# Token sums as split ones products, earlier z gates and 512-token split value products in a hybrid decoder layer on one core

## The chip, the core and the metric

The kernel runs on one core of a Trainium2 chip. The core has a matrix engine (PE; its weight loads are listed apart as PEld), a vector engine (DVE), a scalar engine (ACT), a GpSimd engine (POOL) and a sync engine (SP) that here only issues transfers. Each engine takes its instructions strictly in the order of its own program and waits for the others through semaphores. The metric is device time in microseconds (us) of one execution of the whole layer, as the median of several runs. A profile is one further execution with every instruction's start and duration recorded; L429 means line 429 of the kernel before.

## What is computed

One decoder layer over 2048 tokens of width 1024: RMS norm, one combined projection, three branches, a gated merge, an output projection and the residual. Cut to what the change touches:

```python
kk = heads(k * k_k); kk = kk / max(norm(kk, axis=-1), 1e-12)      # branch A: sum of squares over 64 channels
...
q = rope(rms_norm(q.reshape(t, 8, 64), q_g), pos)                 # branch B: sum of squares over 64 channels
p = softmax(concat([q @ kband.T * 64**-0.5 (masked), sink]))[..., :-1]
y_b = (p @ vband) * silu(z_b)
...
q = rms_norm(q.reshape(t, 4, 128), xq_g)                          # branch C: sum of squares over 128 channels
p = softmax(q @ km.T * 128**-0.5)                                 # 256 memory tokens
y_c = (p @ vm) * silu(z_c)
...
x = x + (g0*(y_a @ Wa) + g1*(y_b @ Wb) + g2*(y_c @ Wc)) @ w_out
```

Branch A is RWKV-7 time mixing with 8 heads of 64 channels, branch B sliding-window attention with 8 query heads, branch C cross attention with 4 heads into 256 memory tokens.

## The kernel before

The sequence is worked in four superblocks of TB = 512 tokens. Activations stand transposed, channels on the 128 partitions and 512 tokens along the free axis, so a sum over a head's channels is a sum over partitions.

All large products are float32 products made of three dense ones (`gemm3`, L425 to L431): each operand is split into a rounded high part and the remainder (type F32R), and high by high, high by low and low by high are accumulated. The high part is an ACT copy, the low part a DVE subtraction. Weights are loaded and split in the first superblock (L411, L412), written back to memory and read in split form (`whl`) later. Products with plain F32 operands (token sums, transposes, attention's probabilities times values, the recurrence) are left to the PE's own float32 path: the trace shows two instructions for each such matmul in the program.

`tok_stat` (L468) makes the sums of squares: for each of the four 128-token tiles the squares are the stationary operand and a narrow matrix of ones (`bones`, 128x2, for two heads of 64; `ones1`, 128x1, for one head of 128) is the moving one. Tokens come out on partitions. It is called once for each pair of heads in `rwkv_prep` (L669), once for each cross head (L899), once for each pair of heads in `swa_pair` (L996), and for the keys. A few narrow DVE instructions carry the sums into place (L673, L901, L998); POOL raises them to the power -0.5 (`rpow`, L398).

`cross_head` (L886) loads the head's keys `km` and values `vm` by SP transfers, projects and splits the queries, makes scores, the softmax with ACT (L918), scales the probabilities (L930), transposes them with PE (L932), copies them out of PSUM with ACT (L934) and multiplies by the values in plain F32, 256 tokens at a time (L936). Then `silu2` projects the z gate (24 dense products, a tanh on ACT, one DVE instruction) and L939 multiplies. `swa_pair` (L982) ends in the same way: transposes (L1042), value products (L1052), then `silu2` (L1056) and the multiplication L1057.

The program is written as two generators, `stream_r` (branch A: preparation, a triangular inverse on DVE, a recurrence of eight steps for two pairs of heads at a time) and `stream_f` (cross heads, window attention, the merges and gates). `weave` interleaves them by the numbers they yield. This only sets ranks: `order` (L276) then lays out every engine's instructions anew. `lay_out` keeps a clock for each engine, gives each instruction a cost by formula (`cost_PE`, `cost_DVE` and so on), lets buffers of a name be taken in program order only when one is free, and among the instructions that could start takes the one of lowest rank. What comes out is a fixed order on PE, DVE, ACT, POOL and SP. Dense projections that wait for nothing fill PE between the links of the dependent work.

Buffers that matter: `g2` (11 of 128x512), `rt` (6), `gt` (2, for gates), PSUM tiles `mm` (2, projections), `rw` (2, branch A), `as_` (2, attention), `oo` (1, attention output).

Of the kernel before, what the change touches and what calls it, by code (L numbers as in the profile page):

```python
# [19 lines left out]
TB = 512  # L20
NG = 11
NRT = 6
SCRATCH = 1024
RAW = 3
C = 64
NC_ = TB // C
# [258 lines left out]
def build(tc, A, nsb=4):  # L285
    nc = tc.nc
# [18 lines left out]
    def g2(dt=F32, shape=(128, TB)):  # L305
        return gp_.tile(list(shape), dt, name="g2")
# [52 lines left out]
    def pcol(name, i=0):  # L359
        o, w = PV[name]  # L360
        return pv[:, o + i:o + i + 1]
# [106 lines left out]
    def tok_stat(sq, nh, ntile, out):  # L468
        rhs = bones if nh == 2 else ones1
        for i in range(ntile):  # L470
            PE.matmul(out[:, i * nh:(i + 1) * nh], sq[:, i * 128:(i + 1) * 128], rhs, start=True, stop=True)
# [4 lines left out]
    V.memset(ones1, 1.0)  # L476

# [61 lines left out]
    Vd = dp.tile([128, 2, 512], F32, name="mv")  # L539
# [9 lines left out]
    def mem_kv(mT):  # L549
# [48 lines left out]
        for i in range(2):  # L598
            t = g2()
            S.activation(t, o[i], AF.Copy)  # L600
            nc.sync.dma_start(Vd[:, i], t)
# [10 lines left out]
    def chunks(t):  # L612
        return t.rearrange("p (c t) -> p c t", t=C)
# [9 lines left out]
    def tmp(tag="rt", bufs=NRT):  # L623
        return rp.tile([128, TB], F32, name=tag, bufs=bufs)
# [5 lines left out]
    def rwkv_prep(p, i, Z, dk, Nc, sb, hT, lwla, group):  # L630
# [35 lines left out]
        sq = tmp()  # L666
        S.activation(sq, k, AF.Square, scale=pcol("k_k", p))
        st = rw_ps()
        tok_stat(sq, 2, 4, st)  # L669
        sums, own = st[:, :8].rearrange("p (a e) -> p a e", e=2), dk[:, i].rearrange("p (a o) -> p a o", o=2)  # L670
        for e, h in ((0, EV), (1, OD)):
            for o, at in ((0, EV), (1, OD)):
                V.tensor_scalar(own[h, :, o], sums[at, :, e], 1e-24, None, op0=ALU.max)  # L673
# [195 lines left out]
    def silu2(blk, hT):  # L869

        o = proj(blk, hT)
        t = g2()
# [13 lines left out]
    def cross_head(h, sb, hT, yh, yl):  # L886
        km = rp.tile([128, 2, M], F32R, name="km", bufs=2)
        nc.sync.dma_start(km.bitcast(F32), Kd[h])
        vm = rp.tile([128, 2, 128], F32, name="vm", bufs=2)
        nc.sync.dma_start(vm, Vd[:, :, h * 128:(h + 1) * 128])  # L890
# [33 lines left out]
        yield 5.667  # L924
        oo = o_ps()
        for t2 in range(2):
            pt = s_ps().rearrange("p (k i t) -> p k i t", k=2, i=2)
            for i in range(2):
                q = 2 * t2 + i
                V.tensor_scalar(prs[t2][:, i], prs[t2][:, i], dn[:, q:q + 1], None, op0=ALU.mult)  # L930
                for kt in range(2):
                    PE.transpose(pt[:, kt, i], prs[t2][:, i, kt * 128:(kt + 1) * 128], ident)  # L932
            pts = g2(shape=(128, 2, 256))
            S.activation(pts.rearrange("p k t -> p (k t)"), pt.rearrange("p k i t -> p (k i t)"), AF.Copy)  # L934
            for kt in range(2):
                PE.matmul(oo[:, t2 * 256:(t2 + 1) * 256], vm[:, kt], pts[:, kt], start=kt == 0, stop=kt == 1)  # L936
        yield 3
        z = silu2(B_ZC + h, hT)
# [43 lines left out]
    def swa_pair(j, sb, hT, yh, yl):  # L982
# [49 lines left out]
        yield 4  # L1032
        Ps = []
# [22 lines left out]
        z = silu2(B_ZB + j, hT)  # L1056
# [245 lines left out]
```

## Time and profile before

| | us |
|---|---|
| median of 3 runs | 2292.9 (2291.53 to 2294.29) |
| the profiled execution | 2291.46 |
| its span, first to last instruction | 2289.7 |
| DVE busy in the span | 1481.7 |
| ACT busy in the span | 901.1 |

The profiled execution's time is 1.8 us more than its span. A PE instruction's listed duration includes the part of the pipeline that overlaps its successor: a dense 512-column product is listed with some 390 ns, yet the next starts about 230 ns later. What a product costs on PE is therefore read from the distance between starts, not from its duration.

### The profile page before, as it was taken

Reading aid. Unit: us, or ns where it says so; the run is one execution under the profiler, and the core shown is the slowest. Engines: PE = TensorE matmul, PEld = TensorE weight load, DVE = VectorE, ACT = ScalarE, POOL = GpSimd, SP = SyncE. Lnnn points to the kernel's source line nnn. Section 1 sums busy time; section 2 is a strip of 40 time slices with the busy share of each in tenths; the row PEclk is TensorE's granted clock in tenths of the full one; section 3 lists DMA queues with packets and bytes.
Section 4 is the critical chain, followed back from the end, with each engine's and each line's share of the span. In section 5 each row is a group of like instructions: output and inputs, shape, how many; then the busy total and the mean of one; then the engine's idle time right before and its main releaser. Section 6 shows DMA issues by size and latency. Waiting matters only on the chain.

```text
span 2289.7 us, 37168 instructions
## 1 busy us (share of the span) xinstructions
PE 2251.8 (98%) x13900; PEld 1832.9 (80%) x13900; DVE 1481.7 (65%) x3798; ACT 901.1 (39%) x1971; POOL 149.5 (7%) x209
## 2 busy tenths in 40 slices
PE   8999999999999999999999999999999999999999
PEld 6878778778788788878888878887887887887887
DVE  7799789774458766953435966784244696686312
ACT  6654564545243443433214344332222434434210
POOL 1000110000000010000000001000000001000000
PEclk9999999999999999999999999999999999999999
DMA  7766556589834344446773433445675434343555
GB/s 241 265 210 230 174 178 222 208 288 335 312 135 159 128 140 152 152 155 232 236 254 125 152 122 135 149 148 186 230 251 184 152 131 165 120 153 117 210 193 192
DMA packets 146227, 430.56 MB, mean 188 GB/s; under 512 B 16641, under 2 KB 21121, under 8 KB 146049
## 3 DMA queue, kind: packets, MB, share of 16 engines
q1 hardware_dynamic: 129920, 398.83, 50.4%
q10 hardware_dynamic: 16128, 29.37, 3.8%
q8 instruction: 110, 1.80, 0.3%
q14 instruction: 69, 0.56, 0.1%
HBM read 333.24 MB, written 94.90 MB: 187 GB/s over the span
## 4 chain that ended last, share of the span: by engine, by line
PE 82%; DVE 10%; DMA 3%; ACT 2%; issue 2%; POOL 2%; SPq 0%; ACTq 0%; DVEq 0%; POOLq 0%
PE mm L429 20%; PE mm L431 20%; PE mm L430 19%; PE rw L706 2%; PE rw L827 1%; DVE whl L412 1%; PE oo L1052 1%; PE rw L820 1%; PE mm L1100 1%; PE oo L936 1%; PE mm L1098 1%; PE mm L1099 1%; PE rw L812 1%; POOL var L398 1%; DMA g<-in_x 1%
## 5 line engine op out<-in xcount | busy, mean ns | idle before, releaser
L429 PE MATMUL mm<-hH,whl 128*128 128x512 f32 x1888 | 753.3, 399 | 0.6 <-ACT gt L1065 0.6
L431 PE MATMUL mm<-hH,whl 128*128 128x512 f32 x1888 | 750.9, 398 | 0.0
L430 PE MATMUL mm<-hL,whl 128*128 128x512 f32 x1888 | 749.1, 397 | 0.0
L431 PEld LDWEIGHTS mm<-hH,whl 128*128 128x128 f32 x1888 | 355.6, 188 | 71.7 <-issue 0.7
L429 PEld LDWEIGHTS mm<-hH,whl 128*128 128x128 f32 x1888 | 355.9, 189 | 70.7 <-ACT gt L1065 1.2
L430 PEld LDWEIGHTS mm<-hL,whl 128*128 128x128 f32 x1888 | 355.7, 188 | 69.1 <-issue 0.5
L411 ACT ACTIVATE whl<-raw 128x512 fp32r<-128x512 f32 x178 | 112.3, 632 | 173.6 <-PE mm L431 98.2
L412 DVE TENSOR_TENSOR whl<-raw,whl 128x512 fp32r<-128x512 f32 x178 | 124.5, 701 | 62.3 <-ACT whl L411 61.2
L429 PE MATMUL mm<-yh,whl 128*128 128x512 f32 x384 | 152.0, 396 | 0.8 <-DVE g L1080 0.7
L430 PE MATMUL mm<-yl,whl 128*128 128x512 f32 x384 | 152.0, 396 | 0.0
L431 PE MATMUL mm<-yh,whl 128*128 128x512 f32 x384 | 150.8, 393 | 0.0
L818 ACT ACTIVATE SP<-Z,Pl 64x64 f32<-64x64 f32 x256 | 89.0, 348 | 117.2 <-DVE Z L828 113.6
L754 DVE STREAM_SHUFFLE ibc<-Nc 128x496 f32<-128x496 f32 (+30 forms) x248 | 113.7, 474 | 0.0
L755 DVE TENSOR_TENSOR ibc<-ibc,Yi 128x496 f32<-128x496 f32 (+30 forms) x248 | 104.9, 423 | 4.2
L1027 ACT ACTIVATE g<-g,mxs,st 128x256 f32<-128x256 f32 (+1 forms) x128 | 74.9, 588 | 79.2 <-DVE mxs L1020 78.9
L1080 DVE SCALAR_TENSOR_TENSOR g<-g,mm 128x512 f32<-128x512 f32 x32 | 21.9, 686 | 128.3 <-PE mm L431 128.3
L756 DVE TENSOR_TENSOR Yi<-Yi,ibc 128x496 f32<-128x496 f32 (+30 forms) x248 | 104.0, 419 | 1.4
L828 DVE SCALAR_TENSOR_TENSOR Z<-rw,Pl,SP 64x64 f32<-64x64 f32 x224 | 63.4, 283 | 44.3 <-PE rw L827 40.7
L429 PEld LDWEIGHTS mm<-yh,whl 128*128 128x128 f32 x384 | 72.1, 188 | 16.9 <-DVE g L1080 1.3
L430 PEld LDWEIGHTS mm<-yl,whl 128*128 128x128 f32 x384 | 72.2, 188 | 14.6
L431 PEld LDWEIGHTS mm<-yh,whl 128*128 128x128 f32 x384 | 72.1, 188 | 14.3
L824 DVE TENSOR_TENSOR Z<-rw,dk 64x128 f32<-64x128 f32 x128 | 36.8, 288 | 64.6 <-PE rw L820 54.5
(1815 smaller groups left out, 3718.3 us busy)
## 6 DMA issues: line engine op xcount, KB each, us to landing
whl<-k SPq DMA_DIRECT2D x486, 512.0 KB, 3.3
k<-whl SPq DMA_DIRECT2D x162, 512.0 KB, 3.2
raw<-in_w_in SPq DMA_DIRECT2D x118, 256.0 KB, 3.7
g<-in_x ACTq DMA_DIRECT2D x32, 256.0 KB, 4.3
out<-g ACTq DMA_DIRECT2D x32, 256.0 KB, 4.0
raw<-in_w_proj SPq DMA_DIRECT2D x24, 256.0 KB, 3.7
rt<-in_x ACTq DMA_DIRECT2D x24, 256.0 KB, 4.9
rt<-in_xt ACTq DMA_DIRECT2D x24, 256.0 KB, 5.7
```

What stands on the lines that cost most here:

```text
L411: S.activation(w[:, 0], raw, AF.Copy)
L412: V.tensor_tensor(w[:, 1], raw, w[:, 0].bitcast(F32), op=ALU.subtract)
L429: PE.matmul(out, lh, rh, start=i == 0, stop=False)
L430: PE.matmul(out, lh, rl, start=False, stop=False)
L431: PE.matmul(out, ll, rh, start=False, stop=i == n - 1)
L706: m = PE.matmul(g[:, c], BK[h, c0 + c], Q[h, c0 + c], start=True, stop=True)
L754: V.stream_shuffle(bc[:, :, :w], N_[:, :, s + 1:], [s] * 32)
L755: V.tensor_tensor(bc[:, :, :w], bc[:, :, :w], Y[:, :, s:s + 1].to_broadcast([128, n, w]), op=ALU.mult)
L756: V.tensor_tensor(Y[:, :, s + 1:], Y[:, :, s + 1:], bc[:, :, :w], op=ALU.add)
L818: S.activation(SP[h, i], Z[h, i, e, c], AF.Copy, scale=g[4][h, c:c + 1])
L828: upds = [V.scalar_tensor_tensor(Sst[h, g[0]] if c == NC_ - 1 else Z[h, i, e, c + 1], pS[h, i, e], g[4][h, c:c + 1], SP[h, i], op0=ALU.mul ...
L1027: S.activation(prs[b][:, i, m0:], prs[b][:, i, m0:], AF.Exp, scale=r2[:, b, i:i + 1], bias=mx[:, b, i:i + 1], accum_out=mx[:, b, 2 + i:3 + i])
```

## The change

Four edits, all inside `build`:

1. In superblocks 1 to 3 (`sb >= FIRST`; the first superblock keeps `tok_stat`) the token sums of `rwkv_prep`, `cross_head` and `swa_pair` become `spread_sums`: the squares are split into high and low (ACT copy, DVE subtraction) and are the moving operand of two dense products of 512 columns with a 128x128 matrix of ones (`ones2` in two blocks of 64, or `onesw`) as the stationary one. Every partition of the PSUM tile then holds the sum. To bring tokens to partitions, `half_sums` multiplies the PSUM tile by an identity pattern (`eye64`) and reduces over each chunk of 64; the cross heads use four `tensor_tensor_reduce` with `ident`. The sums of the sliding window's keys (L960) and of the memory keys stay.
2. In all four superblocks the cross heads' values are kept split (`Vd` and `vm` twice as large, `vm` with one buffer instead of two). The probabilities of all 512 tokens are transposed into two PSUM tiles, split, and multiplied by `gemm3` in six dense products of 512 columns in place of four plain ones of 256.
3. In `cross_head` the z gate's result goes to a `gt` buffer instead of a `g2`.
4. In `swa_pair` `silu2` stands ahead of the transposes in the program, not behind the value products.

```diff
+FIRST = 1
...
+    def spread_sums(out, w, sq, hi, lo):
+        S.activation(hi, sq, AF.Copy)
+        V.tensor_tensor(lo, sq, hi.bitcast(F32), op=ALU.subtract)
+        PE.matmul(out, w, hi, start=True, stop=False)
+        PE.matmul(out, w, lo, start=False, stop=True)
+    def half_sums(d, out, junk):
+        j = chunks(junk)
+        V.tensor_tensor(j, chunks(out), eye64.unsqueeze(1).to_broadcast([128, NC_, 64]), op=ALU.mult)
+        V.tensor_reduce(d, j, axis=AX.X, op=ALU.add)
...
-    Vd = dp.tile([128, 2, 512], F32, name="mv")
+    Vd = dp.tile([128, 2, 2, 512], F32, name="mv")
...
         for i in range(2):
-            t = g2()
-            S.activation(t, o[i], AF.Copy)
-            nc.sync.dma_start(Vd[:, i], t)
+            t = [g2(F32R), g2(F32R)]
+            S.activation(t[0], o[i], AF.Copy)
+            V.tensor_tensor(t[1], o[i], t[0].bitcast(F32), op=ALU.subtract)
+            for u in range(2):
+                nc.sync.dma_start(Vd[:, u, i], t[u].bitcast(F32))
...
         st = rw_ps()
-        tok_stat(sq, 2, 4, st)
+        if sb >= FIRST:
...
+            spread_sums(st, ones2, sq, *(rp.tile([128, TB], F32R, name="rt", bufs=NRT) for _ in range(2)))
+            half_sums(dk[:, i], st, sq)
+            V.tensor_scalar(dk[:, i], dk[:, i], 1e-24, None, op0=ALU.max)
...
-        vm = rp.tile([128, 2, 128], F32, name="vm", bufs=2)
-        nc.sync.dma_start(vm, Vd[:, :, h * 128:(h + 1) * 128])
+        vm = rp.tile([128, 2, 2, 128], F32R, name="vm", bufs=1)
+        nc.sync.dma_start(vm.bitcast(F32), Vd[:, :, :, h * 128:(h + 1) * 128])
...
-        tok_stat(sq, 1, 4, st)
-        V.tensor_copy(rs[:, :4], st[:, :4])
+        if sb >= FIRST:
+            spread_sums(st, onesw, sq, *(g2(F32R), g2(F32R)))
+            for i in range(4):
+                tk = slice(i * 128, (i + 1) * 128)
+                V.tensor_tensor_reduce(sq[:, tk], st[:, tk], ident, 1.0, 0.0, ALU.mult, ALU.add, rs[:, i:i + 1])
...
+        for q in range(4):
+            pr = prs[q // 2][:, q % 2]
+            V.tensor_scalar(pr, pr, dn[:, q:q + 1], None, op0=ALU.mult)
+        pts = []
+        for kt in range(2):
+            pt = s_ps()
+            for q in range(4):
+                PE.transpose(pt[:, q * 128:(q + 1) * 128], prs[q // 2][:, q % 2, kt * 128:(kt + 1) * 128], ident)
+            pts.append((g2(F32R), g2(F32R)))
+            S.activation(pts[kt][0], pt, AF.Copy)
+            V.tensor_tensor(pts[kt][1], pt, pts[kt][0].bitcast(F32), op=ALU.subtract)
         oo = o_ps()
-        for t2 in range(2):
...
-                PE.matmul(oo[:, t2 * 256:(t2 + 1) * 256], vm[:, kt], pts[:, kt], start=kt == 0, stop=kt == 1)
+        gemm3(oo, [((vm[:, 0, kt], vm[:, 1, kt]), pts[kt]) for kt in range(2)])
         yield 3
-        z = silu2(B_ZC + h, hT)
+        z = silu2(B_ZC + h, hT, gp_.tile([128, TB], F32, name="gt", bufs=2))
...
-        tok_stat(sq, 2, 4, st)
-        V.tensor_copy(rs, st[:, :8])
+        if sb >= FIRST:
+            spread_sums(st, ones2, sq, *(g2(F32R), g2(F32R)))
+            d = xp.tile([128, 8], F32, name="dh", bufs=2)
+            half_sums(d, st, sq)
+            for i, h in enumerate((EV, OD)):
+                for o, at in enumerate((EV, OD)):
+                    V.tensor_copy(rs.rearrange("p (b i) -> p b i", i=2)[at, :, i], d.rearrange("p (b o) -> p b o", o=2)[h, :, o])
...
         yield 4
+        z = silu2(B_ZB + j, hT)
         Ps = []
...
         yield 4
-        z = silu2(B_ZB + j, hT)
         V.tensor_tensor(z, ops_, z, op=ALU.mult)
```

The scheduler lays the whole program out anew, so all engines' orders shift a little. Three places show what matters. The first is PE's order at the first pair of heads of branch A in the second superblock, before (`c_bones` is the narrow ones matrix, `rt` the squares, `mm` rows are projections that fill):

```order
L429 MATMUL mm<-hH,whl 128x512
L430 MATMUL mm<-hL,whl 128x512
L431 MATMUL mm<-hH,whl 128x512
L471 MATMUL rw<-c_bones,rt 128x2 x4
L429 MATMUL mm<-hH,whl 128x512
L430 MATMUL mm<-hL,whl 128x512
```

and now (lines of the changed file; L487 is the high part's product, L488 the low part's, L430 to L432 are `gemm3`):

```order
L430 MATMUL mm<-hH,whl 128x512
L487 MATMUL rw<-rt,ones_148 128x512
L431 MATMUL mm<-hL,whl 128x512
L432 MATMUL mm<-hH,whl 128x512
L488 MATMUL rw<-rt,ones_148 128x512
L430 MATMUL mm<-hH,whl 128x512
```

Four narrow float32 matmuls became two dense ones, with two projections set between the high and the low part. The second place is PE's order at the third cross head's value products in the second superblock, before:

```order
L430 MATMUL mm<-hL,whl 128x512
L936 MATMUL oo<-g_7378,vm 128x256 x2
L936 MATMUL oo<-g_7389,vm 128x256 x2
L431 MATMUL mm<-hH,whl 128x512
L429 MATMUL mm<-hH,whl 128x512
```

and now:

```order
L431 MATMUL mm<-hL,whl 128x512
L430 MATMUL oo<-g_7442,vm 128x512
L432 MATMUL mm<-hH,whl 128x512
L430 MATMUL mm<-hH,whl 128x512
L431 MATMUL mm<-hL,whl 128x512
L431 MATMUL oo<-g_7443,vm 128x512
L432 MATMUL oo<-g_7442,vm 128x512
L430 MATMUL oo<-g_7451,vm 128x512
L431 MATMUL oo<-g_7452,vm 128x512
L432 MATMUL oo<-g_7451,vm 128x512
```

Again dense rows stand where float32 rows stood, and projections stand between the first product and those that need the low part. The third place is the fourth cross head of the first superblock, before:

```order
L431 MATMUL mm<-hH,whl 128x512
L932 MATMUL as__1903<-c_ident,g_1893 128x128 x4
L932 MATMUL as__1914<-c_ident,g_1896 128x128 x4
L936 MATMUL oo<-g_1910,vm 128x256 x2
L936 MATMUL oo<-g_1921,vm 128x256 x2
L471 MATMUL as__2124<-c_bones,g_2120 128x2 x4
L429 MATMUL mm<-hH,whl 128x512
```

and now, from where the transposes have ended:

```order
L431 MATMUL mm<-hL,whl 128x512
L430 MATMUL oo<-g_1939,vm 128x512
L432 MATMUL mm<-hH,whl 128x512
L430 MATMUL mm<-hH,whl 128x512
L431 MATMUL mm<-hL,whl 128x512
L431 MATMUL oo<-g_1940,vm 128x512
L432 MATMUL oo<-g_1939,vm 128x512
L430 MATMUL oo<-g_1948,vm 128x512
L431 MATMUL oo<-g_1949,vm 128x512
L432 MATMUL oo<-g_1948,vm 128x512
L472 MATMUL as__2158<-c_bones,g_2154 128x2 x4
L432 MATMUL mm<-hH,whl 128x512
```

Before, transposes and value products followed each other with nothing between; now projections stand between them.

More of the change, by code (lines that the diff above doesn't have):

```diff
@@ L476, in build @@
     V.memset(ones1, 1.0)
+    onesw = bp.tile([128, 128], F32R, name="onesw")
+    S.activation(onesw, ones1.to_broadcast([128, 128]), AF.Copy)
+    eye64 = cp.tile([128, 64], F32, name="eye64")
+    V.tensor_tensor(eye64, ident[:, :64], ident[:, 64:], op=ALU.add)
+    def spread_sums(out, w, sq, hi, lo):
[7 more added lines that the diff above has]
+        V.tensor_reduce(d, j, axis=AX.X, op=ALU.add)
     def bcast_T(out, st, nh, ntile):
@@ L665, in rwkv_prep @@
         yield 10.317
-        sq = tmp()
-        S.activation(sq, k, AF.Square, scale=pcol("k_k", p))
         st = rw_ps()
-        tok_stat(sq, 2, 4, st)
[L670 to L673, printed above, removed]
+        if sb >= FIRST:
+            sq = tmp()
+            S.activation(sq, k, AF.Square, scale=pcol("k_k", p))
+            spread_sums(st, ones2, sq, *(rp.tile([128, TB], F32R, name="rt", bufs=NRT) for _ in range(2)))
+            half_sums(dk[:, i], st, sq)
+            V.tensor_scalar(dk[:, i], dk[:, i], 1e-24, None, op0=ALU.max)
+        else:
+            sq = tmp()
+            S.activation(sq, k, AF.Square, scale=pcol("k_k", p))
+            tok_stat(sq, 2, 4, st)
+            sums, own = st[:, :8].rearrange("p (a e) -> p a e", e=2), dk[:, i].rearrange("p (a o) -> p a o", o=2)
+            for e, h in ((0, EV), (1, OD)):
+                for o, at in ((0, EV), (1, OD)):
+                    V.tensor_scalar(own[h, :, o], sums[at, :, e], 1e-24, None, op0=ALU.max)
         V.reciprocal(dk[:, i], dk[:, i])
@@ L867, in rwkv_chain, with silu2 @@
         yield 10.587
-    def silu2(blk, hT):
+    def silu2(blk, hT, t=None):
         o = proj(blk, hT)
-        t = g2()
+        t = g2() if t is None else t
         S.activation(t, o, AF.Tanh, scale=0.5)
@@ L995, in swa_pair @@
         st = s_ps()
-        tok_stat(sq, 2, 4, st)
         rs = xp.tile([128, 8], F32, name="st8", bufs=2)
-        V.tensor_copy(rs, st[:, :8])
+        if sb >= FIRST:
[5 more added lines that the diff above has]
+                    V.tensor_copy(rs.rearrange("p (b i) -> p b i", i=2)[at, :, i], d.rearrange("p (b o) -> p b o", o=2)[h, :, o])
+        else:
+            tok_stat(sq, 2, 4, st)
+            V.tensor_copy(rs, st[:, :8])
         rpow(rs, rs, 64 * EPS)
```

12 lines of the change are left out of this document (3 added, 9 removed).

## The prediction

> **What bounds the kernel now.** I read the page first, then busy time by superblock, then what PE waits for, then starts on PE around the products that change. The page:
>
> ```profile
> PE 2251.8 (98%) x13900; PEld 1832.9 (80%) x13900; DVE 1481.7 (65%) x3798; ACT 901.1 (39%) x1971; POOL 149.5 (7%) x209
> PE 82%; DVE 10%; DMA 3%; ACT 2%; issue 2%; POOL 2%; SPq 0%; ACTq 0%; DVEq 0%; POOLq 0%
> ```
>
> PE is busy for 98% of the span and holds 82% of the chain that ended last. Overlapping durations make a busy PE look better than it is, so the next view is what its idle time waits for, in the second superblock, and the busy time of each stretch (columns PE, PEld, DVE, ACT, POOL):
>
> ```profile
> PE mm L1100 <- DVE mB L1089: 2.9, 1, 2.9
> PE rw L856 <- DVE rt L853: 0.5, 1, 0.5
> 0.00:580.00 580.00, 553.25 (x3439) 450.23 (x3440) 461.76 (x1138) 316.97 (x665) 50.05 (x74) 0.99 0.68 236
> 580.00:1140.00 560.00, 556.13 (x3440) 452.53 (x3439) 351.85 (x909) 204.81 (x454) 34.09 (x47) 1.00 0.51 177
> 1140.00:1695.00 555.00, 553.37 (x3434) 450.15 (x3434) 341.17 (x891) 196.95 (x441) 34.11 (x47) 1.00 0.51 173
> 1695.00:2290.00 595.00, 589.09 (x3590) 479.96 (x3588) 326.90 (x863) 182.33 (x412) 31.25 (x41) 1.00 0.48 165
> ```
>
> From 580 us on PE idles 2 to 6 us in each superblock, while DVE has some 210 us free in 560 and ACT 355. There, time taken off PE is time taken off the span. In the first superblock PE idles 27 us and DVE is busy 462 of 580; there the two share the bound.
>
> **Token sums** (36 sets: 4 pairs in branch A, 4 cross heads, 4 pairs in branch B, in three superblocks). Starts on PE around one set:
>
> ```profile
> 1196.06 0.39 PE L431 MATMUL mm<-hH,whl 128*128 128x512 f32 x1
> 1196.29 0.95 PE L471 MATMUL rw<-c_bones,rt 128*128 128x2 f32 x8
> 1197.10 0.49 PE L429 MATMUL mm<-hH,whl 128*128 128x512 f32 x1
> 1197.42 0.40 PE L430 MATMUL mm<-hL,whl 128*128 128x512 f32 x1
> 1197.65 0.40 PE L431 MATMUL mm<-hH,whl 128*128 128x512 f32 x1
> ```
>
> A dense product takes 0.23 from start to start (1196.06 to 1196.29, 1197.42 to 1197.65). The set takes 0.81, and the dense product behind it 0.32, that is 0.09 more than usual, the price of coming back from float32. So a set costs 1197.42 - 1196.29 - 0.23 = 0.90, two dense products 0.46: 0.44 saved, 36 x 0.44 = **15.8 us**.
>
> **Value products** (16 heads, all superblocks):
>
> ```profile
> 720.92 0.39 PE L430 MATMUL mm<-hL,whl 128*128 128x512 f32 x1
> 721.15 1.89 PE L936 MATMUL oo<-g,vm 128*128 128x256 f32 x8
> 722.69 0.58 PE L431 MATMUL mm<-hH,whl 128*128 128x512 f32 x1
> 723.11 0.40 PE L429 MATMUL mm<-hH,whl 128*128 128x512 f32 x1
> ```
>
> A head costs 723.11 - 721.15 - 0.23 = 1.73, six dense products 1.38: 0.35 saved, 16 x 0.35 = **5.6 us**.
>
> Both sums take each group to be alone among dense products, so that its return price of 0.09 or more goes with it. In the order of all of PE's rows, a dense row stands directly behind a token sum at 58 places before and 20 now, behind a plain value product at 14 and none: 52 returns gone. Yet such places fall only from 491 to 467 in all, by 24, since 28 reappear behind transposes and links of the recurrence that stood together with other float32 rows before: 28 x 0.09 = **2.5 us back**. Gain on PE: 15.8 + 5.6 - 2.5 = 18.9.
>
> The Trainium skill (TensorE: Matmul & The Clock Gate, section Back-to-back issue gap) gives about 131 ns for each of a stream of 512-column products. The rows above show 0.23, so the trace does not agree; by the page the 168 added products would be 168 x 0.10 = 17 us cheaper and the time about 2257, an estimate I don't use.
>
> **What the other engines pay.** The new instructions have near relatives:
>
> ```profile
> L881 DVE TENSOR_TENSOR yl<-g,yh 128x512 fp32r<-128x512 f32 x32 | 21.8, 688 | 1.6 <-ACT yh L880 1.5
> L711 DVE TENSOR_TENSOR AB<-rw,AB 64x512 f32<-64x512 f32 x32 | 22.0, 686 | 7.6 <-PE rw L706 7.1
> L848 DVE TENSOR_REDUCE var<-rt 128x8 f32<-128x512 f32 x16 | 10.6, 682 | 2.1 <-ACT rt L846 2.1
> L673 DVE TENSOR_SCALAR dk<-rw 64x4 f32<-64x4 f32 x64 | 10.2, 159 | 0.9
> L1015 DVE CUSTOM_DVE_ANT_0 g<-as__2611,amask x2: 285/352/419, 206.0 to 206.5; 128x128 f32<-128x128 f32 x1, 128x256 f32<-128x256 f32 x1
> L1015 DVE DVE_READ_ACCUMULATOR2_ANT mxs<- x128: 73/84/103, 206.2 to 2065.2; 128x1 f32 x128
> L880 ACT ACTIVATE yh<-ya 128x512 fp32r<-128x512 f32 x16 | 9.9, 631 | 0.6
> ```
>
> Branch A: 0.69 to split, 0.69 to multiply out of PSUM, 0.68 to reduce, one clamp for four (-3 x 0.16): 1.6. Branch B: the same three and four small copies for one: 2.5. A cross head: 0.69 and four reductions of 0.285 + 0.084, one copy less: 2.0. A head's values: two splits, 1.4. By superblock DVE gets 4 x (1.6 + 2.5 + 2.0 + 1.4) = 30 us on 352 of 560, 68% in all; ACT 12 x 0.63 = 7.6. What hides this is the dense projections between the links. Without that cover each late low part would stop PE, which is the second rival. I take 0 for superblocks 2 to 4.
>
> **The first superblock** gets only the values: 8 splits and two more for storing them, 10 x 0.69 = 7 us of DVE where it is scarce. Its longest stall stands at the fourth cross head:
>
> ```profile
> 172.61 0.71 PEld L932 LDWEIGHTS as__1903<-c_ident,g 128*128 128x128 f32 x4 [3.89 <-issue]
> 172.64 1.09 PE L932 MATMUL as__1903<-c_ident,g 128*128 128x128 f32 x4 [3.50 <-DVE g L930]
> 69.00:180.00 111.00, 105.37 (x550) 87.25 (x549) 96.41 (x205) 60.09 (x129) 10.18 (x16) 0.95 0.64 219
> 171.80:178.60 6.80, 5.96 (x20) 5.01 (x20) 5.87 (x17) 2.75 (x5) 0.00 (x0) 0.50 0.67 234
> ```
>
> Between 69 and 180 us DVE is busy 96 of 111. At worst all 7 us appear in the span; at best none, since the new order has projections between transposes and values where the old had nothing. I take **2 us lost**, nearer to none for that reason.
>
> **At nothing.** The z gate of branch B moves ahead in the program: its 24 products, its two `whl` transfers on SP, tanh and DVE instruction all move, none is added; it holds a `g2` longer, and `oo` is freed sooner. PE fills with other projections meanwhile; if none were left, its 24 x 0.23 = 5.5 us would stand alone, but they are PE's work in any case. The cross gate's `gt` buffer lies idle in that phase, since gates of the merges come later. The single `vm` buffer adds a wait on SP: the load for a head can't go before the last value product of the head before, and the weight loads stand behind it in the queue.
>
> ```profile
> vm<-mv SPq DMA_DIRECT2D x16, 128.0 KB, 2.5
> ```
>
> It lands in 2.5 us at half the size. The `whl` ring holds eight tiles, each 12 dense products (four by three) long, 2.7 us, so a late issue has cover of several tiles. If that cover were gone, 15 heads x 2.5 = 38 us at most; I take 0, because the new order on SP puts each `vm` among the weight loads at the place where the buffer comes free.
>
> **Sum.** 2291.5 (profiled) - 18.9 + 2 = 2274.6. The median of the runs is 1.4 above that execution, the lowest run equal to it. I forecast **2274**. With the unknowns (returns all saved, +2.5; first superblock from 5 us better to 7 worse; 3 us by chance of a new order) its own range is 2264 to 2282.
>
> **Rivals.**
>
> *The first superblock eats the gain.* The rows show what a late softmax costs there: 3.9 us without PE, and then 6.8 us at a granted clock of 0.50, 3.4 lost: 7.3 a head. The Trainium skill (TensorE: Matmul & The Clock Gate, section HAM oscillation) says that PE idle for more than about 3.4 us falls to half its clock; by that rule the stall would be paid twice, and this trace agrees. If the splits bring it to one more head, the time is 2274 + 7 = 2281; at three more, 2296, which is no change. For it: DVE's 87% there. Against: the projections now between. Chance 0.12, of which 0.04 for no change.
>
> *PE waits for the low part* (slower). PE is strictly in order, and the low part's product stands 2 to 3 products behind the high part's. If DVE were still busy with its inverse, each of the 36 sets would stop PE for the ACT copy and the split, 0.63 + 0.69 = 1.32: 48 us, 2321. From 17 / 36 = 0.47 us a set the gain is gone. The kernel has such a pair already:
>
> ```profile
> L730 PE MATMUL rw<-rt,ones 128*128 128x512 f32 x16 | 6.5, 408 | 0.0
> L731 PE MATMUL rw<-rt,ones 128*128 128x512 f32 x16 | 6.3, 391 | 0.0
> ```
>
> The last column is idle time before them: none in 16 sets, under the same scheduler. Chance 0.08.
>
> *The recurrence sets the end, not PE* (the change then does on PE what it says and gives nothing). Then PE's savings become idle time: about 2291. The second superblock's recurrence ends here, and PE goes on:
>
> ```profile
> 1043.66 0.87 PE rw L856 x8
> 1043.00:1112.00 69.00, 69.00 (x310) 57.20 (x310) 20.59 (x36) 20.89 (x40) 1.21 (x2) 1.00 0.67 226
> ```
>
> PE has 69 us of projections and merges left with no gap, against some 6 us saved in a superblock. Chance 0.05.
>
> *More than the sum*: the 27 us of idle time in the first superblock shrink by 10 or more with the new order: about 2262 or below. Chance 0.09.
>
> **How the numbers follow.** Forecast 0.66, first superblock 0.12, low part 0.08, recurrence 0.05, more 0.09. 0.2% is 4.6 us, about what a measurement of this kernel tells from no change: faster means below 2288.3. That holds for the forecast, "more" and 0.08 of the first rival: 0.83. Same: 0.04 + 0.05 = 0.09. Slower: 0.08. The range runs from 2259 (within "more") to 2288 (most of the first rival).
>
> **What would show it.** PE stays busy for 98% of a shorter span; the two new products of a token sum start 0.23 after one another and their neighbours, with no 0.32 behind them and no idle time before L488 of the changed file. Idle PE time after 580 us should stay below 15 us in total, DVE's busy time rise to about 1580. A first superblock (first 580 us) ending later than before with a new stretch at clock 0.50 speaks for the first rival; idle time before low-part products of 0.5 us each for the second; PE idle between the recurrence's links with equal span for the third. I am wrong if three superblocks together don't become at least 10 us shorter.

## The result and the profile after

| kernel | runs | median us | lowest to highest us | ratio to before, 95% interval |
|---|---|---|---|---|
| before | 6 | 2292.22 | 2288.98 to 2294.29 | 1 |
| changed | 6 | 2284.28 | 2281.06 to 2286.06 | 0.9966 [0.9953, 0.9979] |

The change is faster by 7.9 us, 0.34%. The time lies in the predicted range, but the gain is less than half of the 18 us that were forecast. The profiled execution took 2284.38 us, with a span of 2282.6; 2274.6 had been forecast for it.

The same rows of the page, of the changed kernel (busy time of each engine, and the engines' shares of the chain that ended last):

```profile
PE 2235.9 (98%) x13652; PEld 1804.6 (79%) x13652; DVE 1559.6 (68%) x4001; ACT 919.7 (40%) x2008; POOL 151.0 (7%) x209
PE 68%; DVE 21%; DMA 4%; ACT 3%; issue 2%; POOL 1%; SPq 0%; DVEq 0%; ACTq 0%; POOLq 0%
```

PE's busy share is 98% again. DVE's busy time rose by 78 us, less than the 98 of the forecast (to some 1580). What differs is the chain: PE held 82% of it and holds 68% now, DVE 10% and now 21%. DVE, which was busy for two thirds of the time before and after, has become a part of what sets the end.

PE's waits in the second superblock of the changed kernel (line waiting and releaser; us in total, times, longest):

```profile
PE rw L733 <- DVE QO L721: 0.9, 1, 0.9
PE as__9432 L487 <- ACT g L485: 0.7, 1, 0.7
PE rw L839 <- DVE Z L855: 0.4, 1, 0.4
PE oo L1095 <- ACT g L1087: 0.4, 1, 0.4
PE rw L802 <- issue: 0.3, 1, 0.3
PE mm L430 <- DVE g L1122: 0.2, 1, 0.2
PE as__9950 L488 <- DVE g L486: 0.2, 1, 0.2
PE as__11692 L1140 <- DVE g L1147: 0.2, 1, 0.2
```

The same view of the kernel before has two rows here, of 0.5 and 0.2 us. Now there are eight, and five of them (L733, L487, L839, L1095 and L488) come again at the same lines in the third and the fourth superblock. None is long, and only that at L488 is the wait for a low part of which the second rival spoke. Over the three superblocks 3.0 us of idle time stand at the products of the new sums: 2.4 at L487, nearly all for ACT's copy, and 0.6 at L488.

Short as they are, the page doesn't show all of them. A dense product starts 0.227 us after the one before it, and its record lasts 0.39; so a pause of up to 0.16 between two of them lies inside the first one's record and counts as busy. For the accounts below, each PE instruction of superblocks 2 to 4 is charged with the distance to the next start. That distance is split into: the dense price (0.227 for 512 columns, 0.120 for 256); float32 products and transposes; returns (what the dense product directly behind such an instruction takes beyond its price); hidden pauses (the same beyond-price time behind another dense product); and idle time.

| superblocks 2 to 4, us | before | changed | difference |
|---|---|---|---|
| dense products | 1347.6 | 1380.3 | +32.7 |
| float32 products and transposes | 246.3 | 199.0 | -47.3 |
| returns (365 and 329) | 39.1 | 34.7 | -4.4 |
| **work, sum of the three** | 1633.0 | 1614.0 | **-19.0** |
| hidden pauses | 22.4 | 27.1 | +4.7 |
| idle | 4.6 | 10.3 | +5.7 |
| **waits, sum of the two** | 27.0 | 37.4 | **+10.4** |

The row of hidden pauses isn't all waiting. At some 140 places of both kernels a product on a smaller tile of the matrix engine follows a dense one, and starts 0.10 us later than a dense one would (the median of these places): 13.6 us before and 13.9 now. The difference of 4.7 lies elsewhere: 3.2 of it between two dense products, 1.8 in the last record ahead of a visible wait.

So PE did become 19.0 us cheaper there (17.5 were forecast: 15.8, three quarters of 5.6, less 2.5). Waits took 10.4 of it back. The first superblock, up to its last output product, went from 625.4 to 626.8 us, +1.4.

### The profile page after: what moved, and what is told of

It reads as the page before. It is cut to its first block, busy times and chain, and to the rows that moved or that the text cites. A ratio compares the mean times of both kernels' runs of the same rounds, so it can differ in the third digit from the quotient of the medians.

```text
span 2282.6 us, 36918 instructions
## 1 busy us (share of the span) xinstructions
PE 2235.9 (98%) x13652; PEld 1804.6 (79%) x13652; DVE 1559.6 (68%) x4001; ACT 919.7 (40%) x2008; POOL 151.0 (7%) x209
## 4 chain that ended last, share of the span: by engine, by line
PE 68%; DVE 21%; DMA 4%; ACT 3%; issue 2%; POOL 1%; SPq 0%; DVEq 0%; ACTq 0%; POOLq 0%
PE mm L430 16%; PE mm L432 16%; PE mm L431 16%; DVE whl L413 2%; DVE ibc L781 1%; PE rw L854 1%; PE mm L1142 1%; PE mm L1140 1%; PE mm L1141 1%; PE rw L847 1%; DVE ibc L782 1%; PE rw L839 1%; DVE Yi L783 1%; PE rw L733 1%; DMA raw<-in_w_proj 1%
## 5 line engine op out<-in xcount | busy, mean ns | idle before, releaser
L430 PE MATMUL mm<-hH,whl 128*128 128x512 f32 x1888 | 752.1, 398 | 2.5 <-DVE g L901 1.3
L432 PE MATMUL mm<-hH,whl 128*128 128x512 f32 x1888 | 749.4, 397 | 0.0
L430 PEld LDWEIGHTS mm<-hH,whl 128*128 128x128 f32 x1888 | 355.2, 188 | 74.8 <-issue 1.5
L432 PEld LDWEIGHTS mm<-hH,whl 128*128 128x128 f32 x1888 | 355.2, 188 | 71.2 <-issue 0.5
L430 PE MATMUL mm<-yh,whl 128*128 128x512 f32 x384 | 151.9, 396 | 0.6 <-ACT gt L1107 0.4
L432 PE MATMUL mm<-yh,whl 128*128 128x512 f32 x384 | 151.7, 395 | 0.0
L1107 ACT ACTIVATE gt<-mm 128x512 f32<-128x512 f32 x64 | 37.9, 593 | 128.9 <-PE mm L432 128.7
L430 PEld LDWEIGHTS mm<-yh,whl 128*128 128x128 f32 x384 | 72.2, 188 | 15.6 <-DVE g L1122 0.6
L432 PEld LDWEIGHTS mm<-yh,whl 128*128 128x128 f32 x384 | 72.1, 188 | 14.5
L1069 ACT ACTIVATE g<-g,mxs,st 128x256 f32<-128x256 f32 (+1 forms) x128 | 74.4, 585 | 16.1 <-DVE mxs L1062 14.4
```

The lines of the kernel that those rows point to most:

```text
L430: PE.matmul(out, lh, rh, start=i == 0, stop=False)
L432: PE.matmul(out, ll, rh, start=False, stop=i == n - 1)
L1069: S.activation(prs[b][:, i, m0:], prs[b][:, i, m0:], AF.Exp, scale=r2[:, b, i:i + 1], bias=mx[:, b, i:i + 1], accum_out=mx[:, b, 2 + i:3 + i])
L1107: S.activation(t, gp, AF.Tanh, scale=0.5)
```

## Where the waits stand

Two stretches of 20 us of the second superblock (columns PE, PEld, DVE, ACT, POOL, granted clock, DMA share, GB/s), first of the kernel before:

```profile
840.00:860.00 20.00, 20.00 (x101) 16.82 (x99) 12.30 (x35) 8.48 (x23) 2.85 (x7) 1.00 0.20 70
900.00:920.00 20.00, 20.00 (x123) 16.55 (x123) 15.61 (x41) 7.38 (x18) 1.91 (x2) 1.00 0.37 128
```

and of the changed kernel:

```profile
840.00:860.00 20.00, 19.06 (x96) 15.03 (x94) 18.30 (x30) 7.46 (x12) 2.63 (x6) 1.00 0.14 49
900.00:920.00 20.00, 19.30 (x114) 15.12 (x113) 19.31 (x50) 7.97 (x18) 1.91 (x2) 1.00 0.34 115
```

DVE rose from 12.3 to 18.3 and from 15.6 to 19.3 of 20 us, and there PE waits. In the first of these stretches the change's own DVE rows (L486, L493 and L494, one of each) make 2.1 of the 6.0 us; the rest is older work that the new order has put there. Nor does a full DVE alone stop PE: the kernel before has stretches in which DVE is as full and PE doesn't wait:

```profile
920.00:940.00 20.00, 20.00 (x122) 16.68 (x121) 19.76 (x55) 7.80 (x20) 0.00 (x0) 1.00 0.42 150
940.00:960.00 20.00, 20.00 (x101) 16.97 (x100) 19.70 (x74) 4.52 (x11) 2.65 (x4) 1.00 0.45 159
```

The timeline of the changed kernel in the first of the two stretches, 840 to 860 us (start, duration, engine, line, tiles):

```profile
854.22 0.39 PE L432 MATMUL mm<-hH,whl 128*128 128x512 f32 x1
854.72 0.68 DVE L721 TENSOR_TENSOR QO<-rr__8813,Pt 64x512 f32<-64x512 f32 x1
855.43 0.69 DVE L1119 SCALAR_TENSOR_TENSOR mB<-gt,mm 128x512 f32<-128x512 f32 x1
855.54 0.34 PE L733 MATMUL rw<-QO,BK 64*128 64x128 f32 x1 [0.93 <-DVE QO L721]
```

The product that waits, L733, isn't one of the change's. It needs `QO`, which DVE multiplies late, because it has other work first; in the kernel before, `QO` was ready at 842.5 us and its first product stood at 860.1. PE's order is written out ahead by the planner, so PE stands still whatever is behind this product. Most of the idle time, 7.3 of 10.3 us, stands at old products like this one and not at those of the new sums.

## The experiments

Twelve kernels were run, each with its own runs of the kernel before on the same chip. The table has them all beside the change: the median, the ratio, and against the kernel before the length of the first superblock and, in superblocks 2 to 4, work and waits as split above (from the one profiled execution of each; it lies up to 4 us from the kernel's median, that of sums_and_values 6 us, so these columns are for the places and not for the total).

| kernel | median us (before on its chip) | ratio, 95% interval | first superblock | work, 2 to 4 | waits, 2 to 4 |
|---|---|---|---|---|---|
| the change | 2284.28 (2292.22) | 0.9966 [0.9953, 0.9979] | +1.4 | -19.0 | +10.4 |
| sums_alone | 2295.48 (2291.33) | 1.0021 [1.0012, 1.0030] | +3.9 | -14.4 | +14.2 |
| values_alone | 2297.63 (2291.33) | 1.0029 [1.0017, 1.0040] | +7.2 | -4.2 | +5.1 |
| z_alone | 2298.73 (2291.33) | 1.0033 [1.0021, 1.0044] | -0.4 | +2.0 | +2.2 |
| dve_work_alone | 2298.17 (2291.33) | 1.0029 [1.0017, 1.0040] | +5.0 | +1.2 | +2.8 |
| sums_and_values | 2306.98 (2291.38) | 1.0071 [1.0054, 1.0087] | +6.9 | -12.5 | +27.0 |
| setup_later | 2284.94 (2291.38) | 0.9974 [0.9964, 0.9984] | +2.4 | -19.2 | +8.2 |
| truer_costs | 2277.15 (2291.38) | 0.9939 [0.9927, 0.9951] | +7.6 | -19.9 | -3.2 |
| truer_costs_before | 2300.34 (2291.38) | 1.0038 [1.0026, 1.0050] | +10.4 | -2.1 | +0.7 |
| truer_costs_late | 2272.45 (2289.95) | 0.9923 [0.9909, 0.9936] | +2.7 | -20.1 | -0.9 |
| truer_dve_late | 2269.17 (2289.95) | 0.9911 [0.9897, 0.9924] | +1.9 | -19.9 | -3.7 |
| truer_pe_late | 2275.14 (2289.95) | 0.9936 [0.9924, 0.9949] | +3.5 | -21.7 | +1.9 |
| truer_costs_before_late | 2289.34 (2289.95) | 0.9993 [0.9984, 1.0002] | +2.6 | -2.3 | -0.9 |

**The parts one by one.** Three kernels make one part of the change each (all three have the change's two new constants too), and a fourth gives the kernel before the change's DVE work alone. The token sums alone (values and z gates as before):

```diff
 st = s_ps()
-tok_stat(sq, 1, 4, st)
+if sb >= FIRST:
+    spread_sums(st, onesw, sq, *(g2(F32R), g2(F32R)))
...
```

> The kernel before with the token sums of the change alone (values and z gates as before). By the starts on PE this takes 29.4 us of narrow float32 matmuls and about 3 us of returns off PE and puts 16.4 us of dense ones on: 16 us off. Theory DVE load (the new DVE work makes PE wait from the second superblock on, some 0.1 us of wait for 1 us of DVE work): DVE gets about 73 of the change's 97 us, waits cost 7 to 9, the time is 2283 to 2286. Theory z gates (the waits come from the z gates' new places): 2276 to 2278. Theory new layout (any new order of the engines brings its own waits, whatever the DVE work): anywhere from 2276 to 2290, and the parts of the change don't add up.

The values alone (`vm` and `mv` in two parts, `gemm3` over 512 tokens; sums and z gates as before):

> The kernel before with the value products of the change alone (split values, 512 tokens at a time, one buffer for them). On PE 28.0 us of float32 products go and 21.8 us of dense ones come, with a few returns: 6 to 8 us off. Theory DVE load: 24 us of DVE, waits of 2 to 4, 2286 to 2289. Theory z gates: 2284 to 2286. Theory new layout: 2284 to 2294.

The z gates alone (the gate of branch B ahead of `Ps`, the cross gate in `gt`; sums and values as before):

> The kernel before with the z gates' new places alone. PE, DVE and ACT do the same work as before. Theory DVE load: 2291 to 2293. Theory z gates: 2298 to 2303. Theory new layout: anywhere from 2286 to 2298.

The kernel before with DVE work that nothing reads, about as much as the change adds:

```diff
 tok_stat(sq, 1, 4, st)
+if sb:
+    dve_sums(sq, g2, False)
...
+V.tensor_tensor(g2(), pts.rearrange("p k t -> p (k t)"), pts.rearrange("p k t -> p (k t)"), op=ALU.subtract)
```

> The kernel before with DVE work like that of the change and nothing else: at each token sum from the second superblock on one subtraction, one product and one reduction of 512 columns (cross heads: a subtraction and four reductions of 128), and a subtraction of 512 columns behind each copy of transposed probabilities. Nobody reads the results; PE does the same as before. Theory DVE load: PE waits by 8 to 12 us more from the second superblock on, 2299 to 2304. Theory z gates: 2291 to 2293. Theory new layout: 2286 to 2298, with waits in other places than in the changed kernel.

Each part alone is slower than the kernel before: by 4.2, 6.3 and 7.4 us, 17.9 in sum, where the whole is 7.9 faster. The prices on PE hold all the same: values alone save 4.2 us of work in superblocks 2 to 4 (12 heads x 0.35 = 4.2 forecast), sums alone 14.4 (15.8 forecast). But with the sums alone the waits take 14.2 back. The longest new ones are at the value transposes, here in the second superblock:

```profile
PE as__7710 L963 <- DVE g L961: 1.5, 1, 1.5
PE as__8859 L487 <- ACT g L485: 0.7, 1, 0.7
PE as__7403 L963 <- DVE carry L638: 0.6, 1, 0.6
```

The work that nothing reads raises DVE's busy time between 632 and 2270 us from 996 to 1070 us, where the change has 1071, yet the waits there grow by 2.8 only. So a fuller DVE isn't enough by itself. In the first superblock, where this kernel adds only the eight splits of the values (some 5.5 us by the rows of 0.69), it becomes 5.0 longer. That would be the worst case of the prediction, all of DVE's time in the span; but sums_alone adds no DVE work there beyond a constant and becomes 3.9 longer too, so how much is DVE's time and how much the new order isn't shown.

**The cover.** The change without its two z-gate moves:

```diff
-z = silu2(B_ZC + h, hT, gp_.tile([128, TB], F32, name="gt", bufs=2))
+z = silu2(B_ZC + h, hT)
...
-z = silu2(B_ZB + j, hT)
 Ps = []
...
 yield 4
+z = silu2(B_ZB + j, hT)
```

> The changed kernel with the z gates where they were (token sums and values as in the change). The parts alone were each slower than before, the whole is 8 us faster, so theory DVE load as first put has fallen; two remain. Theory z cover (the z gate's projections, moved ahead, are what PE does while DVE makes the splits; without them the sums and values gain nothing): 2288 to 2296, with 8 us or more of PE waits above the changed kernel's from the second superblock on. Theory full DVE (PE waits where DVE is full for 20 us at a time, whatever the z gates do): 2282 to 2286, with waits as in the changed kernel.

It takes 2306.98 us, 15.6 more than the kernel before and some 23 more than the whole change. The edit that the prediction put down at nothing carries the result: without it there is none, although alone it is a loss of 7.4. The timeline of PE at the fourth cross head of the second superblock, without the moves:

```profile
750.86 0.30 PE L965 MATMUL as__7761<-c_ident,g 128*128 128x128 f32 x1 [1.92 <-DVE g L960]
...
752.57 0.50 PE L430 MATMUL oo<-g,vm 128*128 128x512 f32 x1 [0.58 <-ACT g L967]
753.69 0.79 PE L431 MATMUL oo<-g,vm 128*128 128x512 f32 x1 [0.62 <-DVE g L968]
754.28 0.63 PE L432 MATMUL oo<-g,vm 128*128 128x512 f32 x1
```

and the same head in the changed kernel:

```profile
745.88 0.27 PE L965 MATMUL as__7770<-c_ident,g 128*128 128x128 f32 x1
745.90 0.48 PE L431 MATMUL mm<-hL,whl 128*128 128x512 f32 x1
...
747.36 0.39 PE L430 MATMUL oo<-g,vm 128*128 128x512 f32 x1
747.59 0.39 PE L431 MATMUL mm<-hL,whl 128*128 128x512 f32 x1
747.82 0.39 PE L432 MATMUL mm<-hH,whl 128*128 128x512 f32 x1
748.04 0.39 PE L431 MATMUL oo<-g,vm 128*128 128x512 f32 x1
```

In the change eight projection products stand between the transposes and the low part's value product (six ahead of the first `oo`, two more behind it), and no product waits. Without the moves PE waits 1.92, 0.58 and 0.62 us, with nothing between. Why there is nothing, ACT's rows of the same kernel show:

```profile
751.92 0.60 ACT L967 ACTIVATE g<-as__7761 128x512 fp32r<-128x512 f32 x1 [2.58 <-PE as__7761 L965]
...
752.89 0.60 ACT L900 ACTIVATE g<-mm 128x512 f32<-128x512 f32 x1
753.37 0.62 ACT L990 ACTIVATE g<-mm 128x512 f32<-128x512 f32 x1
753.84 0.71 ACT L992 ACTIVATE g<-mm,c_pv 128x512 f32<-128x512 f32 x1
```

and those of the changed kernel:

```profile
736.17 0.60 ACT L900 ACTIVATE gt<-mm 128x512 f32<-128x512 f32 x1 [3.71 <-PE mm L432]
746.08 0.60 ACT L967 ACTIVATE g<-as__7761 128x512 fp32r<-128x512 f32 x1 [3.72 <-PE as__7761 L965]
...
747.05 0.61 ACT L990 ACTIVATE g<-mm 128x512 f32<-128x512 f32 x1
```

A projection needs one of two `mm` tiles. Without the moves the head's gate and the next projection (`kp`) hold both, finished, and ACT, which reads them at L900, L990 and L992, stands at the copies of the transposes, which wait for DVE. PE can't begin another projection until 754.5, when the last read of `kp` ends. That ACT doesn't read the gate earlier follows from the planner's rule for buffers: its result would take a `g2`, and the `g2` tiles go out in program order, those of the split probabilities first. With a `gt` tile for the result ACT reads the gate at 736.17, ten us before the copies, and one `mm` tile goes round. What follows the wait is paid a second time, as the windows of the kernel without the moves show (the clock is the third number from the end):

```profile
754.00:757.00 3.00, 3.00 (x11) 2.52 (x10) 2.51 (x7) 0.60 (x2) 0.00 (x0) 0.50 0.00 0
757.00:760.00 3.00, 3.00 (x10) 2.52 (x10) 2.28 (x9) 0.58 (x1) 1.85 (x2) 0.50 0.31 90
```

The same wait of 1.9 at L965 stands in the third and in the fourth superblock, and behind each the clock stays low for 10.2 us:

```profile
1313.40:1323.60 10.20, 9.60 (x27) 7.82 (x27) 7.83 (x25) 2.20 (x5) 1.85 (x2) 0.50 0.09 26
1869.80:1880.00 10.20, 9.71 (x29) 7.49 (x28) 8.92 (x29) 3.27 (x6) 1.85 (x2) 0.50 0.05 16
```

This is the mechanism of the prediction's first rival, in superblocks 2 to 4, and the cross gates' new place holds it off. The three stalls are 3.1, 3.1 and 2.4 us of idle time, and the dense products at half clock behind them take 8.6 us above their price: 17 us in all, about as much as this kernel's waits in superblocks 2 to 4 lie above the change's (27.0 against 10.4). Not traced to a place are the 5.5 us by which its first superblock is longer than the change's. The two moves weren't tried apart: what the earlier gate of branch B is worth by itself isn't shown.

**The constants of the setup.** The changed kernel, with `onesw` and `eye64` made just ahead of the first superblock's loop instead of at the start:

> The changed kernel with its two new constants (the 128x128 ones and the identity pattern) made just ahead of the first superblock instead of ahead of the memory tokens' work. Theory setup (the new constants delay the first weight splits by some 3 us; all kernels with them show a wait of 3 us on ACT's split in the first 20 us, those without don't): 2280 to 2282, the wait gone. Theory new layout: 2280 to 2290, no relation.

2284.94 us: no gain, and a first superblock of 627.8. PE's wait for ACT's split in the first 20 us is still there, 2.7 us against 3.5, so the expected theory fell: the new constants aren't what lengthens the start.

**The planner's costs.** The order on each engine comes from the planner's costs. Rows of the changed kernel stand against some of them: the first row is a scan, which the formula holds to occupy DVE for 0.64 us, the second a small copy, planned at 0.10:

```profile
L676 DVE TENSOR_TENSOR_SCAN rt<-smask,rt 128x512 f32<-128x512 bf16 x16 | 19.6, 1224 | 0.4
L1037 DVE COPY st<-dh 64x4 f32<-64x4 f32 x48 | 8.2, 171 | 0.8
```

A dense product of 512 columns is planned at 14 + 0.424 x 512 = 231 ns and starts after 227. DVE is planned too early, PE too late. truer_costs corrects both and changes no instruction:

```diff
-self.busy = 14 + 0.424 * n
+self.busy = 14 + 0.416 * n
...
-self.busy = max(100, self.dur - 85)
+self.busy = max(150, self.dur - 62)
+if type(self.ins).__name__ == 'InstTensorScalarPtr' and getattr(self.ins, 'is_tensor_tensor_scan', False):
+    self.dur, self.busy = 1240, 1140
```

> The changed kernel with the scheduler's costs closer to the trace: a dense product of 512 columns 227 ns instead of 231, DVE's occupancy 23 ns longer for each instruction and at least 150, a scan 1140 instead of 638. No instruction is added or taken away, only the order is laid out anew. Theory plan error (PE waits where the plan has DVE earlier than it is and PE later): 2272 to 2279, waits from the second superblock on at most 6 us. Theory full DVE (there the work itself doesn't fit, order or not): 2282 to 2288. Theory new layout: 2278 to 2292.

The same correction in the kernel before:

> The kernel before with the same corrected costs in its scheduler. Theory plan error: little to gain, since PE waits 5 us in all from the second superblock on: 2288 to 2293. Theory full DVE: 2289 to 2294. Theory new layout: 2285 to 2300.

In superblocks 2 to 4 the changed kernel loses its waits (+10.4 becomes -3.2) and keeps its work (-19.9): 23.1 us less than before. The first superblock becomes 6 us longer. The kernel before gets nothing from it past the first superblock and 10.4 us more in it. The last four kernels apply the correction past the first superblock only:

```diff
+if sb == 1:
+    Step.cut = len(tc.nc.cur_bb.bb.instructions)
...
+Step.late = i >= Step.cut
...
-self.busy = 14 + 0.424 * n
+self.busy = 14 + (0.416 if Step.late else 0.424) * n
```

> The changed kernel; the order is laid out with the corrected costs for instructions past the first superblock alone, and with the old costs in it. No instruction differs. If the waits of superblocks 2 to 4 come from the planned costs there, and the longer first superblock of truer_costs (633 against 627 us) from the corrected costs in the first superblock, then the lengths come together: 626.8, 546.7, 546.1, 544.3, that is 14.5 us below the changed kernel, about 2270 us. If what truer_costs showed was chance of another order, it falls anywhere between 2277 and 2288.

> As truer_costs_late, with the corrected costs of DVE alone (a DVE instruction holds its engine for 150 ns at least and for its duration less 62, a scan for 1140), and PE's dense products as before. If the waits come from DVE being planned too early, this takes most of the 14.5 us: 2270 to 2274. If they come from PE being planned too late (it runs ahead of its plan by 0.5 us in 25), it stays at 2282 to 2286.

> As truer_costs_late, with the corrected cost of PE's dense products alone (227 ns for 512 columns instead of 231), and DVE as before. If the waits come from PE being planned too late, this takes most of the 14.5 us: 2270 to 2274. If they come from DVE being planned too early, 2282 to 2286. If both are needed, the two parts lie each between 2274 and 2282.

> The kernel before with the same correction past the first superblock alone. truer_costs_before changed its superblocks 2 to 4 by -1.5 us in sum, so 2290 to 2292; the change would then be worth some 20 us under like costs. If the correction is good for any kernel, it gains as the changed one does: some 2278.

truer_costs_late comes near the sum of its parts: 2272.45 us, with superblocks of 628.1, 547.3, 547.7 and 544.3. The kernel before stays where it was (0.9993, interval over 1), so the correction is no gift to any kernel: it takes away the waits that the change had brought.

DVE's costs alone do all of it and more, 2269.17. PE's alone go most of the way, 2275.14. The expectation that only one of them would work, and the other stay at 2282 to 2286, fell. A reading that fits is that what the plan gets wrong is how far DVE is behind PE, and that either correction moves that; no run compares the plan's times with the trace's. With both, 2272.45, nothing is added to DVE's alone. truer_dve_late is faster than both kernels of the case, 20.8 us below the kernel before. Its page, and its windows where the change waited, with the one behind the first:

```profile
PE 2231.2 (98%) x13652; PEld 1810.6 (80%) x13652; DVE 1560.3 (69%) x4001; ACT 918.8 (41%) x2008; POOL 154.7 (7%) x209
PE 83%; DVE 10%; DMA 3%; ACT 2%; issue 2%; SPq 0%; ACTq 0%; DVEq 0%
```

```profile
840.00:860.00 20.00, 20.00 (x102) 16.87 (x101) 19.39 (x47) 9.82 (x17) 8.83 (x12) 1.00 0.27 97
860.00:880.00 20.00, 19.09 (x120) 15.28 (x120) 15.20 (x35) 13.87 (x37) 0.00 (x0) 1.00 0.35 111
900.00:920.00 20.00, 20.00 (x118) 16.24 (x117) 18.82 (x51) 6.88 (x16) 2.39 (x2) 1.00 0.40 128
```

The number of instructions is that of the change, DVE is as full in the two stretches in which the change waited (19.4 and 18.8 of 20), and PE doesn't wait in them. The waits aren't all gone: at 867.7 us the next set of the same line (L733 in the change, L737 here) waits 0.7 us for `QE`, nearly as long as L733 did. Gone are those at the new sums and most of the others: idle time in superblocks 2 to 4 falls from 10.3 to 3.3 us and hidden pauses from 27.1 to 20.0. The chain is back at PE 83% and DVE 10%. A full DVE by itself doesn't stop PE; the order decides, and the orders laid out by truer costs wait less.

## Why the prediction was wrong

The step that failed is "What hides this is the dense projections between the links", with "I take 0 for superblocks 2 to 4". It was read from DVE's busy time by superblock: 30 us added to 352 of 560, 68%. The load was not put too low, for DVE got 75 us in the three superblocks and not 90. But 68% is a mean over stretches of which some have 12 of 20 us and others 19, and cover in total says nothing of the place: in 840 to 860 and 900 to 920 us DVE got full, and the order, planned with DVE too early, put links on PE where their results weren't ready. The term measured +10.4 us, 5.7 of it as idle time and 4.7 in pauses inside the records. With the order laid out by truer DVE costs the same term is -3.7, and the time is 2269, below the forecast. The prediction had named a sign of being wrong, three superblocks less than 10 us shorter, and it came: they are 8.6 us shorter. That the time still lies in the range is owed to its width, not to the mechanism. The sum of 2274.6 is also one for the profiled execution; for the median, which lay 1.4 above it, it would have been 2276.

Point by point:

- **Token sums and values on PE: right.** Work of superblocks 2 to 4 fell by 19.0 where 17.5 were forecast. The rows of a new sum in the changed kernel look as was said, with the neighbours 0.23 apart and no 0.32 behind:

```profile
1200.23 0.40 PE L430 MATMUL mm<-hH,whl 128*128 128x512 f32 x1
1200.46 0.40 PE L488 MATMUL as__11962<-g,onesw 128*128 128x512 f32 x1
1200.70 0.39 PE L431 MATMUL mm<-hL,whl 128*128 128x512 f32 x1
1200.93 0.39 PE L432 MATMUL mm<-hH,whl 128*128 128x512 f32 x1
```

- **Returns: right.** They fell from 365 to 329 there, by 4.4 us, and rose from 126 to 138 in the first superblock: 24 fewer in all, as counted from the order.
- **"At nothing", the z gates: wrong.** The same instructions in another place are worth some 23 us: the change without them is 15.6 slower than the kernel before. The prediction noted that the gate of branch B holds a `g2` longer and that `gt` lies idle, and took both as harmless; it didn't ask how long a gate that can't be read holds one of two `mm` tiles, without which no projection can cover the chain of transposes, copy, split and value products.
- **The single `vm` buffer, at nothing: right.** No visible wait of PE past the first superblock names a transfer.
- **First superblock, 2 us lost: near, in part by luck.** Less the four heads' saving, +0.6 was forecast and +1.4 came. But the stall that was to decide it moved. At the fourth cross head it is gone; another has come at links of branch A (waits of 3.0 and 2.2 us at L733). Before, then changed:

```profile
165.00:185.00 20.00, 16.50 (x71) 13.49 (x70) 18.73 (x52) 7.48 (x17) 2.29 (x2) 0.83 0.45 151
300.00:325.00 25.00, 22.18 (x143) 17.76 (x142) 20.21 (x41) 13.00 (x30) 0.85 (x1) 0.93 0.49 169
```

```profile
165.00:185.00 20.00, 18.56 (x93) 14.95 (x92) 19.43 (x50) 12.55 (x24) 2.39 (x2) 1.00 0.63 214
300.00:325.00 25.00, 18.40 (x95) 15.12 (x96) 22.20 (x48) 12.40 (x34) 1.98 (x1) 0.80 0.38 127
```

- **Rivals.** PE waiting for the low part was priced at 1.32 us a set; the 36 sets together show 3.0 us of idle time, most of it for ACT's copy ahead of the high part. The recurrence doesn't set the end: the same work in another order ended 15 us earlier. The first rival's mechanism, a stall that also lowers the clock, is real: sums_and_values shows it (the stall priced there at 3.9 us is 3.5 by PE's own row; 3.9 is that of its weight loads). In the change the cross gates' `gt` buffers hold it off past the first superblock.
- **The sign that would have shown it.** Idle time on PE past the first superblock was to stay below 15 us, and it did, at 10.3. That limit was no help: it left room for most of what was lost, and the hidden pauses don't show in it.

Open stays why the first superblock becomes 8 to 10 us longer under the corrected costs. A part of it shows in the granted clock, which stands at 0.50 there for 20 us in the kernel before and in the change, 27 us in truer_costs and 44 us in truer_costs_before; if half of the added time is lost, that is an estimated 3 us in truer_costs and 12 in truer_costs_before. What brings on these stretches isn't traced. Open is also how much of the 3 to 6 us between truer_dve_late, truer_costs_late and truer_pe_late is the luck of one order over another. That every part alone is slower than the kernel before suggests that such luck has a size of some us here.

## What to carry to other kernels

Where the order of a strict engine is written out ahead, work added to another engine is hidden only if the results that the links need come in time; a mean by stage doesn't show that, and even a full window of 20 us doesn't settle it, so read the waits at the links. After a change in an engine's load, first compare the planner's costs with the durations in the profile: here that was worth 15 us more on the change's 8, and nothing to the kernel before. And before an edit that only moves work is put down at nothing, look which buffers it sets free and who waits for them: it may be the cover of the rest.

## What the runs showed of the hardware

- A pause of PE need not show as idle time. Records of 0.39 us at starts 0.227 apart hide pauses of up to 0.16; in the change 4.7 of the 10.4 us that were lost lay there, and only distances from start to start show them.
- The clock fell to 0.50 after shorter gaps than the one of 3.5 us in PE's row of the prediction. In the kernel without the z moves, waits of 1.92, 0.58 and 0.62 us within 5 us, with short products between them, were followed by 6.8 us at half clock; nearly the same waits in the third and the fourth superblock by 10.2 us. The Trainium skill (TensorE: Matmul & The Clock Gate, section HAM oscillation) speaks of single gaps above some 3.4 us; these rows don't agree, since the longest gap was 1.92.
